# Query blocks of the causal attention from the last pair to the first, and the last product in the same order

## The chip, the cores and the metric

One core of a Trainium2 chip runs the whole program. The metric is the device time of one execution, in microseconds (us); lower is better. The engines are TensorE (PE in the profile, its weight loads PEld), VectorE (DVE), ScalarE (ACT), GpSimd (POOL) and SyncE (SP), which here only issues DMAs.

## What is computed

The program is a hybrid block for 1024 tokens of width 1024: a first block (a gated recurrence, a short convolution and a feed-forward part) and a second block with a latent attention of four heads, a pooling branch, an output product and a layer norm. The change touches only the end of the second block. Cut to that, the reference is:

```
def attend(args):                       # one block of 128 queries, all heads
    s = (einsum(qn, k_nope) + einsum(qr, k_rope)) * scale
    mask = pq[:, None, :, None] >= positions[:, None, None, :]
    p = softmax(where(mask, s, neg), axis=-1)
    return einsum(p, v)
o = lax.map(attend, (qn_b, qr_b, pos_b))
...
y_a = mla_branch(...) * silu(gate_a)
y_b = pool_branch(u_pool, pool_w, pool_scale) * silu(gate_b)
mix = concatenate([y_a, y_b], axis=-1) @ w_out
x = layer_norm(alpha * x + mix, ln_g, ln_b)
```

## The kernel before

Everything up to the attention (both input products, the recurrence, the feed-forward part, the pooling branch and its share of the output product, queries, keys and values of all heads) is left alone by the change. Products are done in three terms, with each operand split into a high and a low part.

`attention` (line 1350 and on) works for positions in order with blocks that see only what they may: query block i (128 queries) of a head sees `seen(i)` = 2 (i // 2 + 1) blocks of keys, so the eight blocks of a head are 256, 256, 512, 512, 768, 768, 1024 and 1024 keys wide. The 32 blocks of four heads are numbered n; a pair of blocks shares one tile of transposed weights. Four functions make a pipeline over n:

- `scores(n)`: five matmuls per 512 keys (three terms of the main part, two of the rotary part) into a PSUM tile; VectorE adds the mask and takes the row maximum (line 1380); ScalarE does the exponential (line 1382).
- `weights(n)`: VectorE's reciprocal of the sum (line 1387) and ScalarE's scaling (line 1388).
- `turn(n)`: one transpose per 128 keys on TensorE (line 1398), the high part by ScalarE (line 1402), the low part by VectorE (line 1403).
- `values(j)` for pair j: three matmuls of 256 columns per 128 keys, then VectorE multiplies by the gate (line 1420), ScalarE and VectorE split the result (lines 1421 and 1422).

The loop runs n from 0 to 36. At each n it issues `scores(n)`, then `values((n - 6) // 2)` at even n from 6 on, `turn(n - 3)` and `weights(n)`. At n % 8 = 1 and 5 it loads the next head's queries and keys and its gate on the SP queue, and at n % 8 = 1 and 4 of heads 1 to 3 it loads and splits rows of the output weights (lines 1446, 105 and 106; two row blocks in head 1, one in heads 2 and 3). From n = 32 on `last_product` makes the output tile of 128 tokens number t = n - 32: 24 matmuls of 512 columns over the four heads, residual and layer norm on VectorE (lines 1487 to 1494, with the small steps of lines 393 to 400), ScalarE (1495) and GpSimd (1496, 1497); the last two tiles go in halves (1500 to 1510). Residual tiles are loaded two ahead, on the SP queue.

PSUM gives four tiles of 1024 columns to all of these. The tiles of 128 x 1024 in SBUF come from a pool of 23 buffers that loads, scores and weights share. A planner orders each engine's instructions at build time from the data and buffers that it expects to be free, with the program's order as priority; the engines then run these lists in order. Masks are made for all blocks, in the order 0 to 7, before a branch on whether the positions are in order; the attention is the body of that branch.

Of the kernel before, what the change touches and what calls it, by code (L numbers as in the profile page):

```python
# [20 lines left out]
P = 128  # L21
# [34 lines left out]
def kernel(ctx: ExitStack, tc: tile.TileContext, I, out):  # L56
# [14 lines left out]
    def U(nm, dt=F32, shape=(P, 1024)):  # L71
        count[0] += 1
        return pools["u"].tile(list(shape), dt, name=f"{nm}_{count[0]}", tag="U", bufs=NU)
# [25 lines left out]
    def f(ap):  # L99
        return ap.bitcast(F32)  # L100
# [977 lines left out]
    def mm_rows(ps, y, w, t, halves=(0, 1)):  # L1078
        for n in halves:
            terms = []  # L1080
            li = (slice(None), slice(t * P, (t + 1) * P))
            ri = (slice(None), slice(n * 512, (n + 1) * 512))
            for e in range(len(y)):
                terms += three(y[e], w[e], li, ri)
            products(ps[:, n * 512:(n + 1) * 512], terms)
# [270 lines left out]
    def attention(causal):  # L1356

        N = 32
        if not causal:
            masks_all()  # L1360

        def seen(i):
            return 2 * (i // 2 + 1) if causal else NT

        sm_t, pt_t, ya, wo, Rt = {}, {}, {}, {}, {}

        def scores(n):
            h, i = divmod(n, 8)
            ps = PS("s")
            qs = (slice(None), slice(i * P, (i + 1) * P))  # L1370
            w = seen(i) * P
            for b in range((w + 511) // 512):
                ks = (slice(None), slice(b * 512, min(w, (b + 1) * 512)))
                terms = three(QN[h], KN[h], qs, ks)
                terms.append((QT[h][qs], KR["w"][0][ks]))
                terms.append((QT[h][qs], KR["w"][1][ks]))
                products(ps[ks], terms)
            s = U("sc")[:, 0:w]
            st = small("st", 4, 4)
            V.tensor_tensor_reduce(s, ps[:, 0:w], masks[causal][i][:, 0:w], 1.0, -3.0e38, ADD, MAX, st[:, 0:1])  # L1380
            V.tensor_scalar(st[:, 1:2], st[:, 0:1], -QK_SCALE, None, MUL)  # L1381
            A.activation(s, s, AF.Exp, scale=QK_SCALE, bias=st[:, 1:2], accum_out=st[:, 2:3])  # L1382
            sm_t[n] = s, st

        def weights(n):
            s, st = sm_t[n]
            V.reciprocal(st[:, 3:4], st[:, 2:3])
            A.activation(s, s, AF.Copy, scale=st[:, 3:4])  # L1388

        def turn(n):  # L1390
            s, _ = sm_t.pop(n)
            if n % 2 == 0:
                pt_t[n // 2] = HT("PT")
            pt = pt_t[n // 2]
            ps = PS("t")
            kb = seen(n % 8)
            for k in range(kb):
                PE.transpose(ps[:, k * P:(k + 1) * P], s[:, k * P:(k + 1) * P], ident)  # L1398
            v = ps.rearrange("p (k q) -> p k q", k=8)[:, 0:kb]
            hi = pt[:, 0:kb, (n % 2) * P:(n % 2 + 1) * P]  # L1400
            lo = pt[:, 0:kb, 256 + (n % 2) * P:256 + (n % 2 + 1) * P]
            A.copy(hi, v)
            V.tensor_tensor(lo, v, f(hi), SUB)  # L1403

        def values(j):
            h, q = divmod(j, 4)
            pt = pt_t.pop(j)
            ps = PS("o")
            terms = []
            for k in range(seen(2 * q)):  # L1410
                li = (slice(None), k, slice(h * P, (h + 1) * P))
                vh, vl = VV[0][li], VV[1][li]
                ph, pl = pt[:, k, 0:256], pt[:, k, 256:512]
                terms += [(vh, ph), (vh, pl), (vl, ph)]
            products(ps[:, 0:256], terms)
            qs = slice(q * 256, (q + 1) * 256)
            g = GA[h][:, qs]
            if q == 0:
                ya[h] = U("yah", F32R), U("yal", F32R)
            V.tensor_tensor(g, g, ps[:, 0:256], MUL)  # L1420
            A.copy(ya[h][0][:, qs], g)
            V.tensor_tensor(ya[h][1][:, qs], g, f(ya[h][0][:, qs]), SUB)

        def gate_load(h):
            GA[h] = U("ga")
            SY.dma_start(GA[h], GA_d[h])

        def head_load(h):
            QN[h], KN[h], QT[h] = (U("qn", F32R), U("qn", F32R)), (U("kn", F32R), U("kn", F32R)), U("qt", F32R)
            for t, src in ((KN[h][0], KN_d[h][0]), (QN[h][0], QN_d[h][0]), (KN[h][1], KN_d[h][1]),  # L1430
                           (QN[h][1], QN_d[h][1]), (QT[h], QT_d[h])):
                SY.dma_start(f(t), src)

        gate_load(0)
        for n in range(N + 5):
            if n % 8 == 1 and n // 8 < 3:
                head_load(n // 8 + 1)
            if n % 8 == 5 and n // 8 < 3:
                gate_load(n // 8 + 1)
            if n < N:  # L1440
                scores(n)
                if n % 8 == 1 and n // 8 >= 1:
                    h = n // 8
                    for e in ([0, 1] if h == 1 else [h]):
                        t = U("wo2")
                        SY.dma_start(t, w_out2[e * P:(e + 1) * P, :])
                        wo[e] = t
                if n % 8 == 4 and n // 8 >= 1:
                    h = n // 8
                    for e in ([0, 1] if h == 1 else [h]):  # L1450
                        wo[e] = split(wo[e], "wo2", of=UV if e == 0 else U)
            if n >= 6 and n % 2 == 0:
                values((n - 6) // 2)
            if 3 <= n < N + 3:
                turn(n - 3)
            if n < N:
                weights(n)
            if N - 2 <= n < N:
                t = n - (N - 2)
                Rt[t] = U("rt")  # L1460
                SY.dma_start(Rt[t], R3_d[t])
            if n == N - 2:
                gB, bB = g_bcast(I["ln_g_2"][0, :], "lng"), g_bcast(I["ln_b_2"][0, :], "lnb")
            if n >= N:
                last_product(n - N, ya, wo, Rt, gB, bB)
        for t in range(5, NT):
            last_product(t, ya, wo, Rt, gB, bB)

    def last_product(t, ya, wo, Rt, gB, bB):
        if t + 2 < NT and t + 2 not in Rt:  # L1470
            Rt[t + 2] = U("rt")
            SY.dma_start(Rt[t + 2], R3_d[t + 2])
        r = Rt[t]
        last = t >= NT - 2
        y, w = [ya[h] for h in range(4)], [wo[h] for h in range(4)]
        if t == NT - 1:
            ps = [PS("o2"), PS("o2")]
            for n in range(2):
                mm_rows(ps[n], y, w, t, (n,))
        else:  # L1480
            ps = [PS("o2")] * 2
            mm_rows(ps[0], y, w, t)
        bs = small("bs", 12, 2)
        st = small("lst", 8, 2)
        halves = [slice(0, 512), slice(512, 1024)]
        for h, hs in enumerate(halves):
            V.tensor_tensor(r[:, hs], r[:, hs], ps[h][:, hs], ADD)  # L1487
            V.bn_stats(bs[:, 6 * h:6 * h + 6], r[:, hs])
        V.bn_aggr(st[:, 0:2], bs)
        v, inv, tmp, nb = st[:, 2:3], st[:, 3:4], st[:, 4:6], st[:, 6:7]  # L1490
        V.tensor_scalar(v, st[:, 1:2], LN_EPS, None, ADD)
        if not last:
            rsqrt_col(v, inv, tmp)
            V.scalar_tensor_tensor(nb, st[:, 0:1], -1.0, inv, MUL, MUL)
            A.activation(r, r, AF.Identity, bias=nb, scale=inv)  # L1495
            G.tensor_tensor(r, r, gB, MUL)  # L1496
            G.tensor_tensor(r, r, bB, ADD)
            SY.dma_start(out[0, t * P:(t + 1) * P, :], r)
        else:
            A.activation(tmp[:, 0:1], v, AF.Sqrt)  # L1500
            V.scalar_tensor_tensor(r[:, halves[0]], r[:, halves[0]], st[:, 0:1], gB[:, halves[0]], SUB, MUL)
            newton(v, inv, tmp)
            V.scalar_tensor_tensor(r[:, halves[1]], r[:, halves[1]], st[:, 0:1], gB[:, halves[1]], SUB, MUL)  # L1503
            for hs in halves:
                if t == NT - 1:
                    V.scalar_tensor_tensor(r[:, hs], r[:, hs], inv, bB[:, hs], MUL, ADD)
                else:
                    A.activation(r[:, hs], r[:, hs], AF.Copy, scale=inv)
                    G.tensor_tensor(r[:, hs], r[:, hs], bB[:, hs], ADD)
                SY.dma_start(out[0, t * P:(t + 1) * P, hs], r[:, hs])  # L1510


    second.run(pooled_begin, lambda: kr_product(kr["w"]))
# [32 lines left out]
    with ordered.Else():  # L1546
        attention(False)
# [27 lines left out]
```

## Time and profile before

| | us |
|---|---|
| median of 3 runs | 1722.47 (1722.11 to 1723.81) |
| the profiled execution | 1726.95 |
| its span, first to last instruction | 1725.2 |
| TensorE matmul busy in it | 1627.0 (94%) |
| VectorE busy | 1195.2 (69%) |
| ScalarE busy | 777.0 (45%) |
| GpSimd busy | 359.4 (21%) |
| mean granted TensorE clock | 0.981 |

All positions in time are us from the span's start. A timeline row gives the start, the duration, the engine, the line and operation, output and input tiles with their shapes, how often, and in brackets the idle time in front with what ended it. Matmul durations overlap; how fast TensorE goes is read from the distance of their starts. The attention and the last product fill the span from about 1559 us on.

### The profile page before, as it was taken

To read this page: it belongs to the slowest core of one execution; us is meant where nothing else is said; L and a number is where in the kernel's file an instruction comes from. 1 tells how busy PE (TensorE), PEld (TensorE's weight loads), DVE (VectorE), ACT (ScalarE), POOL (GpSimd) and SP (SyncE) were. 2 spreads that over 40 slices of the span, in tenths; PEclk is the share of its full clock that TensorE was granted. 3 is DMA by queue.
4 is the path that set the end of the run, shared out by engine and by line. 5 is a ranking of instruction groups with operands and counts; after the bars stand their busy time and mean duration, and the time that the engine had idled before them with its cause. 6 is when DMAs were issued, how large, how long until landed. Compare 5 with 4: busy or idle time off the path is not lost. (4 is left out here: it accounts for less than half of the span.)

```text
span 1725.2 us, 20241 instructions
## 1 busy us (share of the span) xinstructions
PE 1627.0 (94%) x7347; PEld 1334.4 (77%) x7347; DVE 1195.2 (69%) x1765; ACT 777.0 (45%) x1147; POOL 359.4 (21%) x347
## 2 busy tenths in 40 slices
PE   5999899999999999999999999999989999988996
PEld 4777677778887787888888888888877878766885
DVE  6977676876498797767677664454877675476767
ACT  6556665762065444444444421120645344035861
POOL 1323333202032322223222000010222220030015
PEclk7999999999999999999999999999999999988998
DMA  9747566288056877877774872420387657766333
GB/s 239 136 78 140 119 122 122 46 332 205 3 149 112 191 146 153 164 148 146 142 162 93 299 269 98 104 42 2 130 159 155 140 110 269 234 195 232 110 111 112
DMA packets 272816, 255.38 MB, mean 148 GB/s; under 512 B 18398, under 2 KB 238404, under 8 KB 272708
## 3 DMA queue, kind: packets, MB, share of 16 engines
q1 hardware_dynamic: 168244, 186.80, 33.7%
q0 software_dynamic: 103744, 65.03, 26.1%
q10 hardware_dynamic: 720, 2.18, 0.3%
q8 instruction: 60, 0.98, 0.2%
q14 instruction: 48, 0.39, 0.1%
HBM read 199.56 MB, written 52.82 MB: 146 GB/s over the span
## 5 line engine op out<-in xcount | busy, mean ns | idle before, releaser
L112 PE MATMUL o<-yw 128*128 128x512 f32 x1632 | 375.9, 390 | 0.0
L112 PEld LDWEIGHTS o<-yw 128*128 128x128 f32 x1632 | 305.6, 188 | 63.7 <-DVE yw L540 0.8
L580 DVE TENSOR_TENSOR x<-x,o 128x512 f32<-128x512 f32 x160 | 108.8, 685 | 136.3 <-PE o L112 136.1
L539 ACT CAST yw<-yraw 128x1024 fp32r<-128x1024 f32 x34 | 35.7, 1051 | 194.9 <-PE o L112 176.3
L412 ACT ACTIVATE xn<-x 128x1024 f32<-128x1024 f32 x24 | 25.5, 1063 | 60.7 <-DVE x L580 54.1
L540 DVE TENSOR_TENSOR yw<-yraw,yw 128x1024 fp32r<-128x1024 f32 x34 | 41.5, 1221 | 14.9 <-ACT yw L539 14.8
L540 DVE TENSOR_TENSOR yw<-wraw,yw 128x1024 fp32r<-128x1024 f32 x34 | 41.5, 1220 | 0.8 <-ACT yw L539 0.8
L1496 POOL TENSOR_TENSOR rt<-rt,lng 128x1024 f32<-128x1024 f32 x6 | 14.4, 2403 | 122.6 <-ACT rt L1495 122.6
L775 DVE TENSOR_TENSOR ffc<-ffc,ffc 128x1024 f32<-128x1024 f32 x24 | 29.4, 1225 | 13.5 <-ACT ffc L772 13.5
L539 ACT CAST yw<-wraw 128x1024 fp32r<-128x1024 f32 x34 | 35.7, 1050 | 6.2 <-DMA wraw<-in_w_out_dram 3.2
L772 ACT ACTIVATE ffc<-ffc 128x1024 f32<-128x1024 f32 x24 | 25.5, 1062 | 25.6 <-DVE ffc L769 25.6
L441 PE MATMUL T<-cst,xn 128*128 128x128 f32 x128 | 19.6, 306 | 17.7 <-DVE ss L422 9.5
L258 POOL DMA_DIRECT2D wu3s<-in_w_in_dram x1 | 1.3, 1282 | 166.5 <-DMA wu3s<-in_w_in_dram 166.5
L1382 ACT ACTIVATE sc<-sc,st 128x256 f32<-128x256 f32 (+3 forms) x32 | 26.3, 824 | 18.9 <-DVE st L1381 18.8
L112 PE MATMUL wob<-yw 128*128 128x512 f32 x144 | 34.1, 389 | 0.0
L112 PE MATMUL o<-PT,Vh 128*128 128x256 f32 x160 | 30.0, 286 | 3.5 <-DVE PT L1403 2.9
L441 PEld LDWEIGHTS T<-cst,xn 128*128 128x128 f32 x128 | 16.5, 157 | 21.2 <-ACT hraw L456 9.9
L112 PEld LDWEIGHTS wob<-yw 128*128 128x128 f32 x144 | 27.0, 188 | 5.6
L422 POOL TENSOR_SCALAR ss<-ss 128x1 f32<-128x1 f32 x16 | 4.5, 281 | 126.0 <-ACT ss L413 125.8
L1380 DVE CUSTOM_DVE_ANT_0 sc<-s,mask 128x256 f32<-128x256 f32 (+3 forms) x32 | 25.9, 819 | 6.3 <-PE s L112 5.8
L672 POOL TENSOR_TENSOR i<-i,xc 128x1024 f32<-128x1024 f32 x8 | 21.2, 2651 | 40.7 <-ACT i L671 36.2
L1398 PE MATMUL t<-cst,sc 128*128 128x128 f32 x160 | 23.3, 277 | 6.6 <-ACT sc L1388 6.1
(1385 smaller groups left out, 4455.3 us busy)
## 6 DMA issues: line engine op xcount, KB each, us to landing
GY<-ffc SPq DMA_DIRECT2D x24, 512.0 KB
yraw<-GY SPq DMA_DIRECT2D x24, 512.0 KB
wraw<-in_w_down_dram SPq DMA_DIRECT2D x24, 512.0 KB
x<-in_x_dram SPq DMA_DIRECT2D x16, 512.0 KB
yraw<-Y SPq DMA_DIRECT2D x12, 512.0 KB
wraw<-in_w_out_dram SPq DMA_DIRECT2D x12, 512.0 KB
Y<-i SPq DMA_DIRECT2D x8, 512.0 KB
R<-x SPq DMA_DIRECT2D x8, 512.0 KB
```

The source lines that it names most:

```text
L112: PE.matmul(ps, lhsT=l, rhs=r, start=(first and j == 0), stop=(last and j == n - 1), skip_group_check=not first)
L412: A.activation(xn, X[t], AF.Square, accum_out=ss[:, 0:1])
L441: PE.transpose(ps[:, k * P:(k + 1) * P], src[:, c * P:(c + 1) * P], ident)
L539: A.copy(s[:, j], src)
L540: V.tensor_tensor(s[:, j + 1], src, f(s[:, j]), SUB)
L580: V.tensor_tensor(X[t][:, ns], X[t][:, ns], ps, ADD)
L672: G.tensor_tensor(i, i, st.pop("xc"), MUL)
L772: A.activation(st["g"], st["g"], AF.Gelu_apprx_tanh)
L775: V.tensor_tensor(st["u"], st["u"], st["g"], MUL)
L1380: V.tensor_tensor_reduce(s, ps[:, 0:w], masks[causal][i][:, 0:w], 1.0, -3.0e38, ADD, MAX, st[:, 0:1])
L1382: A.activation(s, s, AF.Exp, scale=QK_SCALE, bias=st[:, 1:2], accum_out=st[:, 2:3])
L1398: PE.transpose(ps[:, k * P:(k + 1) * P], s[:, k * P:(k + 1) * P], ident)
```

## The change

`block(n)` maps the place n % 8 in a head to the block that is done there: 6, 7, 4, 5, 2, 3, 0, 1. Scores, turns and value products take their block from it, so each head goes from its last pair of query blocks to its first. The last product takes its token tiles in the same order, and the loads of the residual and the stores of the output follow. The loop, what it issues at each n, and all shapes of a block stay as they are.

```diff
+        def block(n):
+
+            return 2 * (3 - n % 8 // 2) + n % 2
+
         def scores(n):
-            h, i = divmod(n, 8)
+            h, i = n // 8, block(n)
...
-            kb = seen(n % 8)
+            kb = seen(block(n))
...
         def values(j):
-            h, q = divmod(j, 4)
+            h, q = j // 4, 3 - j % 4
...
-            if q == 0:
+            if j % 4 == 0:
                 ya[h] = U("yah", F32R), U("yal", F32R)
...
+        def r_load(t):
+            Rt[t] = U("rt")
+            SY.dma_start(Rt[t], R3_d[block(t)])
...
             if N - 2 <= n < N:
-                t = n - (N - 2)
-                Rt[t] = U("rt")
-                SY.dma_start(Rt[t], R3_d[t])
+                r_load(n - (N - 2))
...
-                last_product(n - N, ya, wo, Rt, gB, bB)
+                last_product(n - N, block(n - N), ya, wo, Rt, r_load, gB, bB)
         for t in range(5, NT):
-            last_product(t, ya, wo, Rt, gB, bB)
+            last_product(t, block(t), ya, wo, Rt, r_load, gB, bB)

-    def last_product(t, ya, wo, Rt, gB, bB):
+    def last_product(t, i, ya, wo, Rt, r_load, gB, bB):
+
         if t + 2 < NT and t + 2 not in Rt:
-            Rt[t + 2] = U("rt")
-            SY.dma_start(Rt[t + 2], R3_d[t + 2])
+            r_load(t + 2)
...
-                mm_rows(ps[n], y, w, t, (n,))
+                mm_rows(ps[n], y, w, i, (n,))
...
-            mm_rows(ps[0], y, w, t)
+            mm_rows(ps[0], y, w, i)
...
-            SY.dma_start(out[0, t * P:(t + 1) * P, :], r)
+            SY.dma_start(out[0, i * P:(i + 1) * P, :], r)
...
-                SY.dma_start(out[0, t * P:(t + 1) * P, hs], r[:, hs])
+                SY.dma_start(out[0, i * P:(i + 1) * P, hs], r[:, hs])
```

## Rows read from the trace of the kernel before

**Rows 1.** The page, the chain that ended last, shares of the span by engine.

```profile
PE 11%; DVE 4%; ACT 1%; DMA 1%; issue 1%; POOL 0%; DVEq 0%; ACTq 0%
```

**Rows 2.** Busy time by stretch: PE, PEld, DVE, ACT, POOL, PE clock, DMA, GB/s.

```profile
1569.40:1576.00 6.60, 5.61 (x17) 4.54 (x18) 3.55 (x16) 3.15 (x10) 0.00 (x0) 0.50 1.03 416
1580.00:1660.00 80.00, 76.01 (x517) 68.57 (x516) 58.07 (x156) 65.52 (x121) 0.00 (x0) 1.00 0.20 68
1660.00:1701.00 41.00, 41.00 (x215) 35.05 (x214) 29.51 (x70) 15.08 (x22) 19.20 (x8) 1.00 0.48 167
```

**Rows 3.** Timeline of TensorE, from the last key products to the third value product.

```profile
1552.28 0.79 PE L112 MATMUL kn<-lkvh,wkvh 128*128 128x512 f32 x1 [3.19 <-DVE knl L106]
...
1555.73 0.40 PE L112 MATMUL kn<-lkvh,wkvl 128*128 128x512 f32 x1
...
1559.36 0.28 PE L112 MATMUL s<-knh,qnh 128*128 128x256 f32 x1
...
1569.47 0.69 PE L1398 MATMUL t<-cst,sc 128*128 128x128 f32 x2 [6.08 <-ACT sc L1388]
...
1579.92 0.40 PE L112 MATMUL o<-PT,Vh 128*128 128x256 f32 x2
...
1590.97 0.50 PE L112 MATMUL o<-PT,Vh 128*128 128x256 f32 x2 [1.45 <-DVE PT L1403]
```

**Rows 4.** Timeline of VectorE and ScalarE at the attention's start.

```profile
1567.42 0.42 DVE L1380 CUSTOM_DVE_ANT_0 sc<-s,mask 128x256 f32<-128x256 f32 x1 [0.56 <-DVE mask L1318]
...
1568.07 0.51 ACT L1382 ACTIVATE sc<-sc,st 128x256 f32<-128x256 f32 x1 [6.20 <-DVE st L1381]
...
1570.60 0.42 DVE L1403 TENSOR_TENSOR PT<-t,PT 128x256 fp32r<-128x256 f32 x1 [1.73 <-ACT PT L1402]
1570.94 0.41 DVE L1380 CUSTOM_DVE_ANT_0 sc<-s,mask 128x256 f32<-128x256 f32 x1
```

**Rows 5.** The chain of waits in order of time: start, us, what; whole blocks.

```profile
1577.76 2.32 PE s L112 x10
...
1593.38 0.87 PE t L1398 x8
...
1597.42 2.88 PE o L112 x24
```

**Rows 6.** Groups by line and form from 1566 us on: busy, mean ns, idle before.

```profile
L1380 DVE CUSTOM_DVE_ANT_0 sc<-s,mask 128x1024 f32<-128x1024 f32 x8 | 9.8, 1221 | 2.1 <-PE s L112 2.0
L1403 DVE TENSOR_TENSOR PT<-t,PT 128x1024 fp32r<-128x1024 f32 x8 | 9.8, 1221 | 1.9 <-ACT PT L1402 1.9
L1388 ACT ACTIVATE sc<-sc,st 128x1024 f32<-128x1024 f32 x8 | 9.2, 1146 | 0.2 <-DVE st L1387 0.2
L1382 ACT ACTIVATE sc<-sc,st 128x1024 f32<-128x1024 f32 x8 | 9.2, 1144 | 3.0 <-DVE st L1381 3.0
...
L1402 ACT CAST PT<-t 128x1024 fp32r<-128x1024 f32 x8 | 8.0, 1000 | 0.8 <-PE t L1398 0.8
...
L1403 DVE TENSOR_TENSOR PT<-t,PT 128x768 fp32r<-128x768 f32 x8 | 7.6, 952 | 0.5 <-ACT PT L1402 0.5
L1388 ACT ACTIVATE sc<-sc,st 128x768 f32<-128x768 f32 x8 | 7.5, 939 | 0.5 <-DVE st L1387 0.5
...
L1402 ACT CAST PT<-t 128x768 fp32r<-128x768 f32 x8 | 6.3, 784 | 0.0
...
L106 DVE TENSOR_TENSOR wo2l<-wo,wo2h 128x1024 fp32r<-128x1024 f32 x4 | 4.9, 1213 | 0.0
...
L105 ACT CAST wo2h<-wo 128x1024 fp32r<-128x1024 f32 x4 | 4.2, 1047 | 0.2 <-PE t L1398 0.2
```

**Rows 7.** Timeline of the tail: GpSimd and VectorE.

```profile
1703.91 2.39 POOL L1497 TENSOR_TENSOR rt<-rt,lnb 128x1024 f32<-128x1024 f32 x1
...
1704.36 1.95 DVE L398 TENSOR_TENSOR lst<-lst 128x1 f32<-128x1 f32 x1
```

**Rows 8.** The SP queue: the store of the last residual tile.

```profile
1489.65 0.34 SPq L1158 DMA_DIRECT2D RR<-rx  x1
```

## The prediction

> **What bounds the kernel now.** I read the chain of waits first: it is spread thinly, and its largest share is TensorE at 11% [rows 1], so no single place carries the kernel; only the attention and the last product are touched, so the reading goes on there alone. Next the busy time by stretch. From 1660 us to 1701 us TensorE has no idle time at all, from 1580 to 1660 it is busy 76.01 of 80 us, and from 1569.4 to 1576 its granted clock is 0.50, which is the lower of its two levels, 1.2 GHz [rows 2]. So this stage is bound by TensorE with two leaks: a start that costs much, and 4.0 us of gaps later. The timeline of TensorE shows both. It begins the scores at 1559.36 and waits 6.08 us at 1569.47 for the first softmax; and the third value product of the next head waits 1.45 us at 1590.97 for the split weights [rows 3]. The timeline of VectorE says why the start is late: the first score block is read at 1567.42, behind the masks and the branch, and nothing that this change moves lies ahead of that [rows 4].
>
> **What the change does to the work.** Each head has eight score blocks, of widths 256, 256, 512, 512, 768, 768, 1024, 1024. After the change the widest come first. Nothing is added or removed: the instructions of a head are the same ones in another order, on every engine. I take four places.
>
> **A, the start.** The milestone is the first value product, 1579.92 in the trace [rows 3]. In program order seven score blocks and three turns (the transposes) stand ahead of it in both kernels. A widest score block is ten matmuls in 2.32 us, eight transposes take 0.87, a value product of 24 takes 2.88 [rows 5]; the other sizes go in proportion, so scores cost 0.58, 1.16, 1.74, 2.32 and turns 0.22, 0.44, 0.66, 0.87. Before: 2 x 0.58 + 2 x 1.16 + 2 x 1.74 + 2.32 + 2 x 0.22 + 0.44 = 10.2 us of work, so 1579.92 - 1559.36 - 10.2 = 10.4 us are lost. After: 2 x 2.32 + 2 x 1.74 + 2 x 1.16 + 0.58 + 2 x 0.87 + 0.66 = 13.4 us of work ahead of the same milestone. When does that come? VectorE reads block 0 from 1567.42 as before. There, from that start of 0.42 us to the exponential is 0.65 us [rows 4]; with 1.22 for the wide block [rows 6] it is 1.45, so ScalarE begins at 1568.87. Ahead of the value product it does two wide exponentials (1.14), two wide scalings (1.15), two exponentials and a scaling of width 768 (0.94 each, by the scaling's row) and two splits (1.00) [rows 6]: 2.28 + 2.30 + 2.82 + 2.00 = 9.4 us, to 1578.3; VectorE's low part of the second block, 1.22, ends at 1579.5. Lost: 1579.5 - 1559.36 - 13.4 = 6.7 us. Gain 10.4 - 6.7 = 3.7 us. TensorE fills its early wait with scores that run on to about 1559.36 + 8.1 = 1567.5, and then idles some 4 us instead of 6.08; an idle time of 3.19 us was already enough for the lower clock at 1552.28 [rows 3], so I count on slow matmuls here too, and they fit: from 1571.5 to 1579.5 stand 5.3 us of work. The upper end of the gain is 4.6: the exponential of the fourth block gives way, 0.94 us. The lower end is 0.5, and it hangs on the order in which VectorE was given its work. In the trace it sat idle 1.73 us and did the low part of block 0 at 1570.60, and only then block 1, at 1570.94 [rows 4], though that block's scores had long been made. If this order is kept, block 0 is through only at about 1575.6 (1571.5, transposes at the lower clock 1.75, split 1.00, low part 1.22, issue), block 1 needs 1.45 + 1.14 + 0.3 + 1.15 + 0.87 + 1.00 + 1.22 = 7.1 more, the milestone is 1582.7 and the gain 10.4 - 9.9 = 0.5. I take 3.7, because that idle time holds a place for block 1 once block 0 takes twice as long.
>
> **B, the later heads.** The 4.0 us of gaps between 1580 and 1660 [rows 2] come where a value product finds its weights unsplit. Before, the tightest is the third pair (width 768): between its turn and its product TensorE has 0.58 + 0.87 + 1.16 = 2.6 us of other work, against a split of 0.78 and a low part of 0.95 [rows 6]; it waited 1.45, so 2.6 + 1.45 - 1.73 = 2.3 us of queue lay in front. After, the tightest is the widest pair, four steps into its head: 1.16 + 0.66 + 0.58 = 2.4 us of cover against 1.00 + 1.22 = 2.2. With the same queue it would wait 2.1, with none 0. The queue is shorter (a 512-wide exponential and a gate copy, where a 1024-wide scaling stood), so I take 1.5 us of it: a wait of 1.3, three times (heads 1 to 3; head 0 is in A): 3.9 - 4.0 = -0.1 us. Ends: -4.0 (no waits) and 3 x 2.1 - 4.0 = +2.3. The splitting of the output weights stands in the same step of a head, now a thin one, and is counted in a rival.
>
> **C, the end of the attention.** At step 32 the value product of the third-to-last pair (768 wide) follows its turn by one narrow score block and one turn only, 0.58 + 0.44 = 1.0 us, as no scores are left; it needs 0.78 + 0.95 = 1.7 and some handing over. I take +1.0, between 0 (other products fill it) and 2.0. Before, this place held a narrow pair and 2.32 us of scores, and no gap [rows 2].
>
> **D, the tail.** The last product takes the tiles in the new order with the same shapes, so its cost is unchanged: TensorE has no gap there [rows 2]. Behind it VectorE's small multiply (line 398) waits on a running GpSimd instruction, 1.95 us at 1704.36 while one of 2.39 us ran from 1703.91 [rows 7]; the pace of the tiles ahead of that shifts, so this can be 1.9 us less or 2.4 more, and I take 0. The loads of the residual tiles on the SP queue are the same eight in the same places; the last of those tiles was stored at 1489.65 [rows 8], so which one comes first costs nothing.
>
> Sum: -3.7 - 0.1 + 1.0 + 0 = -2.8 us. Against the profiled execution's own 1726.95 that is 1724.15; on the median, 1722.47 - 2.8 = 1719.7 us. The two differ by 4.5 us before, so I carry the difference, not the level.
>
> **The rivals.** *Gaps gone* (faster): the widest pair comes while two wide score blocks of its own head still cover it, and C is filled by the last product: A and B at -3.7 and -4.0, C at 0, -7.7 us, 1714.8. For it: ScalarE is busy 65.5 of 80 us [rows 2], so it has room when the load is level. Against: its load is not level, the 2.4 us of cover is the thinnest of either order. *Start unchanged*: VectorE keeps block 1 behind block 0's low part, as in the trace [rows 4]; A is -0.5 and the sum +0.4, 1722.9: the change then does not do what it could. *Thin step* (slower): the splitting of the output weights, 1.05 on ScalarE and 1.21 on VectorE [rows 6], falls in front of the widest pair's split in each of heads 1 to 3. A wait is then 1.3 + 1.05 + 1.21 = 3.6 us, B is 3 x 3.6 - 4.0 = +6.7, the sum +4.0, 1726.5. It decides from 2.2 us a head, where 3 waits eat 4.0 + 3.7 - 1.0. *Thin step and a slow clock*: if these waits reach the 3.19 us behind which the trace shows the lower clock, each is followed by what 1552.28 to 1555.73 shows, eight matmuls in 3.45 us where they take 1.86 at full clock, 1.6 us more [rows 3, 5]. B is 3 x (3.2 + 1.6) - 4.0 = +10.4, the sum +7.7, 1730.2. Against it: after the wait of 1.45 us the clock stayed at 1.00 [rows 2, 3].
>
> On that last one the Trainium skill, page "TensorE: Matmul & The Clock Gate", section "HAM oscillation — how this bites in real kernels", speaks against the change: idle stretches that return between bursts of matmuls let the clock be throttled each time, and every burst pays the slow beginning again. By that rule the time would be the 1730.2 of this rival if the waits are long enough; by the row of 1.45 us they cost only themselves.
>
> **How the numbers follow.** Forecast 0.38, gaps gone 0.26, start unchanged 0.16, thin step 0.14, thin step with slow clock 0.06. A measurement of this kernel can tell about 0.2%, 3.4 us, from no change, so the bounds are 1719.0 and 1725.9. The forecast's own spread (1.5 us, mostly A's and D's) puts a third of it under 1719.0: faster 0.26 + 0.12 = 0.38, slower 0.20, same 0.42. The range runs from 1714.0 to 1727.0, over all but the slow clock and the edges of the others; the forecast's own is 1717.5 to 1722.
>
> **What would show it.** A: the first value product near 1579.5 with 13.4 us of work ahead of it, and VectorE reading block 1 before block 0's low part. B: one wait of about 1.3 us in each later head, on the low part of the widest pair. C: about 1 us between the last turns. D: VectorE's tail behind the last matmul as long as now, some 13 us. The prediction is wrong if the weight splits queue ahead of the widest pair, if the waits reach 2.2 us a head, or if TensorE's clock falls after the start.

## The result, and the profile after

The changed kernel took 1738.76 us (median of 4 runs, 1733.71 to 1739.61) beside 1722.29 us (median of 4, 1721.38 to 1723.81) for the kernel before. The measured ratio is 1.0080, with a 95% interval of 1.0064 to 1.0096; the quotient of the two medians, 1.0096, lies at the upper end of it. The change is slower by 0.8%, where 1719.7 us and a range up to 1727.0 were forecast.

The profiled execution of after took 1733.71 us (span 1731.9, mean granted clock 0.976), 6.8 us more than the one of before. That difference is not the cost of the change. After began its first score at 1553.62, before at 1559.36 [rows 3], and no part of the change lies ahead of that point. In the runs of the experiments, the kernel before itself ranged from 1720.6 to 1735.4 us (two executions of it, at mean granted clocks of 0.745 and 0.839, took 2055.4 and 1845.2 us and are left out). So from here on I compare *stages*: from the first score matmul to the end of the span, in each profile. In that measure the same waits come back with the same length, to a tenth or two of a us, in every kernel that leaves the place alone. What does not come back alike is how long the granted clock stays low at the start. In the old order it is back at 1.00 between 14.7 us (e4, below) and 17.9 us (e6) after the first score, 16.7 in before; in the new one between 20.3 us (e5) and 23.7 us (e9), 21.7 in after. Where two kernels differ only in steps behind the matmuls, the part up to the last matmul still differs by 0.5 to 0.8 us (after and e5, e1 and e9, e4 and e10, before and e8, in the table of experiments). So differences of stages under about 1 us are not read as effects.

| us | before | after |
|---|---|---|
| first score matmul to last matmul's start | 152.01 | 162.09 |
| last matmul's start to the end (tail) | 13.83 | 16.19 |
| stage | 165.84 | 178.28 |

The stage grew by 12.4 us: 10.1 on TensorE's side and 2.4 in the tail. That lies inside the measured interval of the whole time (+11.0 to +16.5 us). What the medians differ by beyond it, some 4 us, the profiles do not place.

The page's chain of waits, shares of the span by engine, still names no single place; TensorE's share went from 11% [rows 1] to 12%:

```profile
PE 12%; DVE 4%; ACT 2%; issue 1%; DMA 0%; POOL 0%; DVEq 0%; ACTq 0%
```

Busy time by stretch of after (us, then PE, PEld, DVE, ACT, POOL with their counts, granted clock, DMA share, GB/s), to be laid beside [rows 2]:

```profile
1569.40:1576.00 6.60, 4.54 (x19) 3.58 (x18) 2.15 (x9) 6.60 (x12) 0.00 (x0) 0.55 0.52 197
1600.00:1610.00 10.00, 5.14 (x31) 4.76 (x30) 6.35 (x14) 8.03 (x16) 0.00 (x0) 0.83 0.00 0
1610.00:1620.00 10.00, 10.00 (x68) 9.12 (x67) 5.90 (x15) 6.23 (x12) 0.00 (x0) 1.00 0.68 254
1630.00:1640.00 10.00, 6.88 (x37) 6.55 (x36) 4.97 (x11) 5.64 (x10) 0.00 (x0) 0.67 0.16 52
1640.00:1650.00 10.00, 10.00 (x64) 8.93 (x63) 7.43 (x20) 7.04 (x15) 0.00 (x0) 0.99 0.19 55
1650.00:1660.00 10.00, 9.78 (x69) 8.80 (x67) 7.61 (x23) 9.09 (x14) 0.00 (x0) 1.00 0.00 1
1670.00:1700.00 30.00, 30.00 (x144) 25.17 (x143) 21.89 (x49) 8.54 (x15) 14.24 (x6) 1.00 0.49 177
```

Two of these stretches carry the loss. From 1600 to 1610 TensorE is busy 5.14 us and from 1630 to 1640 6.88 us, and in both the granted clock is below 1.00. Before had 1.00 from 1580 to 1660 [rows 2]. The stretches between and behind them are full or nearly so.

The timeline of all engines in these two places (start, duration, engine, line and operation, tiles and shapes, count; in brackets the idle time in front and what ended it). The lines of weights and turns have moved by four against the kernel before: 1402 is the turn, 1406 and 1407 its high and low part:

```profile
1601.56 1.98 ACT L105 CAST wo2h<-wo 128x1024 fp32r<-128x1024 f32 x2
1602.62 2.36 DVE L106 TENSOR_TENSOR wo2l<-wo,wo2h 128x1024 fp32r<-128x1024 f32 x2 [0.77 <-ACT wo2h L105]
1603.74 1.00 ACT L1406 CAST PT<-t 128x1024 fp32r<-128x1024 f32 x1
1605.23 1.22 DVE L1407 TENSOR_TENSOR PT<-t,PT 128x1024 fp32r<-128x1024 f32 x1
1606.51 0.79 PE L112 MATMUL o<-PT,Vh 128*128 128x256 f32 x2 [4.86 <-DVE PT L1407]
...
1610.74 0.49 PE L1402 MATMUL t<-cst,sc 128*128 128x128 f32 x3
...
1630.55 1.03 ACT L105 CAST wo2h<-wo 128x1024 fp32r<-128x1024 f32 x1
1631.62 1.23 DVE L106 TENSOR_TENSOR wo2l<-wo,wo2h 128x1024 fp32r<-128x1024 f32 x1 [0.77 <-ACT wo2h L105]
1631.80 1.00 ACT L1406 CAST PT<-t 128x1024 fp32r<-128x1024 f32 x1
1633.10 1.22 DVE L1407 TENSOR_TENSOR PT<-t,PT 128x1024 fp32r<-128x1024 f32 x1
1634.46 0.77 PE L112 MATMUL o<-PT,Vh 128*128 128x256 f32 x2 [3.12 <-DVE PT L1407]
...
1639.72 0.58 PE L1402 MATMUL t<-cst,sc 128*128 128x128 f32 x2
```

Read the two groups from top to bottom. On ScalarE, and then on VectorE, the splitting of the output weights (wo2h, wo2l) is done ahead of the split of the widest pair's second block (PT), which TensorE is waiting for. Each of the two engines works its list in order, and VectorE even idles 0.77 us for wo2h with the PT step standing behind it. TensorE's value product of 24 matmuls then waits 4.86 us in head 1, where two row blocks are split, and 3.12 us in head 2, where there is one. And the product itself is slow: 1606.51 to 1610.74 is 4.23 us and 1634.46 to 1639.72 is 5.26 us, where it takes 2.88 at full clock [rows 5].

### The profile page after: what moved, and what is told of

Same layout as the page of the kernel before. It is cut to its first block, busy times and chain, and to the rows that moved or that the text cites. A ratio compares the mean times of both kernels' runs of the same rounds, so it can differ in the third digit from the quotient of the medians.

```text
span 1731.9 us, 20245 instructions
## 1 busy us (share of the span) xinstructions
PE 1632.6 (94%) x7347; PEld 1339.6 (77%) x7347; DVE 1202.8 (69%) x1765; ACT 777.4 (45%) x1147; POOL 359.0 (21%) x347
## 5 line engine op out<-in xcount | busy, mean ns | idle before, releaser
L112 PE MATMUL o<-PT,Vh 128*128 128x256 f32 x160 | 33.7, 307 | 9.5 <-DVE PT L1407 9.3
L112 PEld LDWEIGHTS o<-PT,Vh 128*128 128x128 f32 x160 | 28.4, 212 | 11.4 <-DVE PT L1407 7.0
L441 PE MATMUL T<-cst,xn 128*128 128x128 f32 x128 | 20.1, 310 | 16.9 <-ACT ws0op L267 9.4
L1386 ACT ACTIVATE sc<-sc,st 128x1024 f32<-128x1024 f32 (+3 forms) x32 | 26.3, 824 | 21.0 <-DVE st L1385 19.2
L1407 DVE TENSOR_TENSOR PT<-t,PT 128x1024 fp32r<-128x1024 f32 (+3 forms) x32 | 26.1, 820 | 8.0 <-ACT PT L1406 7.8
L1384 DVE CUSTOM_DVE_ANT_0 sc<-s,mask 128x1024 f32<-128x1024 f32 (+3 forms) x32 | 26.1, 820 | 6.6 <-PE s L112 6.0
```

The source lines that it names most:

```text
L112: PE.matmul(ps, lhsT=l, rhs=r, start=(first and j == 0), stop=(last and j == n - 1), skip_group_check=not first)
L441: PE.transpose(ps[:, k * P:(k + 1) * P], src[:, c * P:(c + 1) * P], ident)
```

## The experiments

All times are stages as above, each from one profile, unless a ratio is given; a ratio is to the kernel before on the same chip, with its 95% interval. Kernels with "one run" have no ratio.

| kernel | first score to last matmul | tail | stage | ratio |
|---|---|---|---|---|
| before | 152.01 | 13.83 | 165.84 | 1 |
| after | 162.09 | 16.19 | 178.28 | 1.0080 |
| e1, weight splits moved | 153.31 | 15.80 | 169.11 | 1.0018 [0.9999, 1.0037] |
| e2, only heads 1 and 2 reversed | 156.31 | 13.81 | 170.12 | 1.0029 [1.0006, 1.0052] |
| e3, only head 0 reversed | 156.26 | 14.08 | 170.34 | 1.0042 [1.0021, 1.0062] |
| e4, only head 3 and the tiles reversed | 151.49 | 16.17 | 167.66 | 1.0033 [1.0009, 1.0057] |
| e5, after with small steps rewritten | 161.39 | 13.13 | 174.52 | one run |
| e6, before with splits moved | 151.76 | 13.82 | 165.58 | one run |
| e7, e1 with a later first split | 154.91 | 15.91 | 170.82 | one run |
| e8, before with small steps rewritten | 152.46 | 13.24 | 165.70 | 1.0006 [0.9992, 1.0019] |
| e9, e1 and e5 together | 154.04 | 12.81 | 166.85 | 0.9998 [0.9982, 1.0014] |
| e10, e4 and e5 together | 152.26 | 13.13 | 165.39 | 0.9988 [0.9972, 1.0003] |

**e1: the weight splits away from the thin step.** In the changed kernel, one line:

```diff
-                if n % 8 == 4 and n // 8 >= 1:
+                if n % 8 == 7 and n // 8 >= 1:
```

> The changed kernel, with the splitting of the output weights moved three steps on, from n % 8 = 4 to n % 8 = 7, behind the widest pair's value product. Theory 1 (the splits stand in front of the widest pair's own split): the waits of 4.9 and 3.1 us at the third head's turn fall under 1.5 us, the granted clock stays at 1.00 from 1590 us on, and 8 to 11 us come back: about 1725 to 1730 us. Rival (the cover of 2.4 us is too thin by itself, splits or not): the waits stay above 3 us and the time within 3 us of the changed kernel's 1738.8.

The stage fell by 9.2 us, from 178.28 to 169.11. The widest pair of head 1, in the timeline of e1:

```profile
1603.26 1.00 ACT L1406 CAST PT<-t 128x1024 fp32r<-128x1024 f32 x1
1604.29 1.22 DVE L1407 TENSOR_TENSOR PT<-t,PT 128x1024 fp32r<-128x1024 f32 x1 [0.30 <-ACT PT L1406]
1604.32 0.39 PE L112 MATMUL o<-PT,Vh 128*128 128x256 f32 x1 [1.26 <-ACT PT L1406]
```

and its busy time by stretch there:

```profile
1604.00:1610.00 6.00, 5.47 (x42) 5.14 (x43) 4.34 (x7) 5.76 (x12) 0.00 (x0) 1.00 0.03 3
```

With no weight split in front, the wait is 1.26 us (and 0.22 more behind it) instead of 4.86, head 2's is 0.67 and 0.57 instead of 3.12, and the granted clock stays 1.00. What the theory expected (waits under 1.5 us, the clock at 1.00, 8 to 11 us back) came, and the rival, that the cover is too thin with or without the splits, fell. The place of the splits is the cause of most of the loss, shown by moving them alone.

**e2, e3, e4: one place of the change at a time.** The order is reversed only for the heads in a list:

```diff
-            return 2 * (3 - n % 8 // 2) + n % 2
+            return 2 * (3 - n % 8 // 2) + n % 2 if n // 8 in (1, 2) else n % 8
...
-            h, q = j // 4, 3 - j % 4
+            h, q = j // 4, block(2 * j) // 2
```

with (0,) in e3 and (3,) in e4; the last product's tiles follow head 3.

> The kernel before, with heads 1 and 2 alone from the last pair to the first; heads 0 and 3 and the last product as before. Theory 1 puts most of the loss here: 6 to 12 us slower than before, 1728 to 1734. Rival (the loss is spread over the start, the heads and the tail alike): 2 to 5 us slower.

> The kernel before, with head 0 alone from the last pair to the first. By the trace of the changed kernel the start lost 11.6 us against 10.4 before: 0 to 2 us slower than before. By the prediction's term A it would be 3.7 us faster.

> The kernel before, with head 3 alone from the last pair to the first, and the last product in that order. Theory: the value products leave the stretch of the last product, its tiles come every 5.4 to 6 us, and VectorE with its waits on GpSimd falls behind: 13.6 us between the last matmul and the end become 15.5 to 16.5, and with some 1 us of waits in head 3 it is 2 to 4 us slower than before. Rival (the tail is the same, the loss lies in the heads alone): at most 1 us slower, and 13.6 us stay 13.6.

The stages grew by 4.3, 4.5 and 1.8 us: 10.6 together, where the whole change costs 12.4. Three expectations on the sizes missed. Theory 1 put 6 to 12 us on heads 1 and 2, and the 4.3 of e2 lies in its rival's 2 to 5. Head 0 was to cost 0 to 2 us and cost 4.5, and e4's 1.8 is under its 2 to 4. So the sum comes near, but not place by place. Head 1 waits only 2.31 us in e2, with the same two row blocks split ahead of it. The difference that e2 keeps is head 0 in the old order, whose last value product, just ahead of this place, has 24 matmuls (2.88 us) instead of 6 (0.72); that these 2.2 us make most of the 2.55 us of difference is argued, not shown. The timeline of e2, and under it its busy time by stretch (the granted clock is the third number from the end):

```profile
1610.97 0.50 PE L112 MATMUL o<-PT,Vh 128*128 128x256 f32 x2 [2.31 <-DVE PT L1407]
```

```profile
1611.00:1612.10 1.10, 1.10 (x9) 1.10 (x10) 1.10 (x3) 0.00 (x0) 0.00 (x0) 1.00 0.00 0
1612.10:1615.30 3.20, 3.20 (x18) 3.20 (x18) 1.17 (x7) 2.32 (x6) 0.00 (x0) 0.52 0.00 0
```

Even a wait of 2.31 us was followed by the lower of the two clock levels, 1.1 us after the matmuls had begun again. In e3 the shape of the loss is another. The reversed head 0 is followed by a head 1 in the old order, and that head waits 0.98, 2.07 and 1.85 us (timeline, and busy time by stretch under it):

```profile
1609.95 0.63 PE L1402 MATMUL t<-cst,sc 128*128 128x128 f32 x4 [2.07 <-DVE st L1384]
...
1620.86 0.50 PE L112 MATMUL o<-PT,Vh 128*128 128x256 f32 x2 [1.85 <-DVE PT L1407]
```

```profile
1609.90:1613.00 3.10, 3.05 (x16) 2.49 (x17) 2.88 (x9) 2.39 (x5) 0.00 (x0) 1.00 0.00 0
1620.80:1624.00 3.20, 3.14 (x27) 3.14 (x28) 2.87 (x10) 1.62 (x5) 0.00 (x0) 1.00 0.26 101
```

The clock stayed at 1.00 there. This change from the new order to the old does not occur in after, where head 1 is reversed too, so e3 does not price the start alone, and that the three sum to near 12.4 is partly chance. In e4, TensorE's part is 0.5 us shorter than before, which the start explains: its clock was back 2.0 us earlier, and its first value product came 19.77 us after the first score instead of 20.56. The waits add up to 10.9 us in e4 and 11.0 in before. The tail of e4 is that of after, 16.17 us, as its theory expected. So the longer tail belongs to the order of head 3 and the tiles, and to nothing ahead of it.

**e6: the same place in the old order.** The kernel before with the splits issued at n = 16 (two row blocks), 24 and 28:

```diff
-                if n % 8 == 4 and n // 8 >= 1:
-                    h = n // 8
-                    for e in ([0, 1] if h == 1 else [h]):
+                if n in (16, 24, 28):
+                    for e in {16: [0, 1], 24: [2], 28: [3]}[n]:
```

> The kernel before, in its own order, with the splitting of the output weights moved from the fifth block of a head to the first block of the next (n = 16, 24; the last at 28), which is the thin step of that order. Theory 1 (the place of the splits in front of a tight pair's own split does the damage, not the order of the blocks): TensorE's waits of 1.45 us at the second and 0.6 us at the third change of heads grow to 2.5 to 4 us each, 3 to 6 us from the first score to the end, more if the clock falls. Rival (only the widest pair suffers): less than 1 us.

No wait of before grew by more than 0.02 us, and the 1.45 us of head 1's third pair are gone. The tightest place of head 0 is as in [rows 3]:

```profile
1591.05 0.50 PE L112 MATMUL o<-PT,Vh 128*128 128x256 f32 x2 [1.44 <-DVE PT L1403]
```

The waits behind it are 0.26, 0.50 and 0.51 us, and the stage is 165.58. But the edit moved only two of the four splits in time. ScalarE began them at 1596.03, 1610.80, 1636.38 and 1645.22; in before at 1595.94, 1598.67, 1625.45 and 1645.89, so the planner left the first and the last where they were. The two that moved (1610.80 and 1636.38) stand near the third pairs of heads 1 and 2, each with one row block, and those pairs did not wait longer. So that a split stands in a step with little cover was not enough by itself in these two places. The general form of the theory fell there, on one profile; two row blocks in one such step of the old order were not tried. What e1 shows holds for the reversed order.

**e7: the first split behind the second exponential.** e1, and in head 0 only:

```diff
+            if n == 0:
+                with tc.issue_after(exps[1]):
+                    A.copy(hi, v)
+            else:
+                A.copy(hi, v)
```

> The changed kernel with the weight splits at n % 8 = 7, and ScalarE's high part of block 0 queued behind the exponential of block 1 instead of ahead of it. Theory for the start (in the changed kernel ScalarE sat 2.06 us in front of that high part while block 1 waited): the first value product comes 1 to 2.5 us earlier after the first score than the 25.0 us of the run with the splits moved. Rival (the start is set by the slow clock and by the amount of work on ScalarE): within 0.5 us of 25.0.

The second matmul of the first value product came 26.58 us after the first score, 1.6 later than in e1 (25.01), so theory and rival both missed. The two profiles also differ in the clock, as the busy time by stretch shows from 21.2 to 24.3 us after the first score (e1, then e7):

```profile
1576.49:1579.59 3.10, 2.69 (x21) 2.32 (x20) 1.96 (x8) 2.85 (x6) 0.00 (x0) 1.00 0.69 190
1583.88:1586.98 3.10, 3.10 (x13) 2.70 (x12) 1.66 (x3) 2.33 (x4) 0.00 (x0) 0.50 0.49 172
```

The clock was low until 24.4 us in e7 and until 21.1 in e1. Between after and e5, whose starts are the same program, a low clock until 21.7 instead of 20.3 us goes with a first value product at 25.26 instead of 24.14 us. So the 1.6 us are no measure of the edit. The gain of 1 to 2.5 us did not show; that ScalarE's order plays no part at all is not shown.

**e5 and e8: the small steps at the end.** The Newton steps of the layer norm (one number for each of 128 tokens) take two operands from SBUF. Written with one, and the other as a column of scalars, in after (e5) and in before (e8):

```diff
-        V.tensor_tensor(tmp[:, 1:2], out, v, MUL)
-        V.scalar_tensor_tensor(tmp[:, 1:2], tmp[:, 1:2], -0.5, out, MUL, MUL)
-        V.scalar_tensor_tensor(out, tmp[:, 1:2], 1.5, out, ADD, MUL)
+        V.tensor_scalar(tmp[:, 1:2], out, v, None, MUL)
+        V.tensor_scalar(tmp[:, 1:2], tmp[:, 1:2], -0.5, out, MUL, MUL)
+        V.tensor_scalar(out, tmp[:, 1:2], 1.5, out, ADD, MUL)
...
-            V.scalar_tensor_tensor(nb, st[:, 0:1], -1.0, inv, MUL, MUL)
+            V.tensor_scalar(nb, st[:, 0:1], -1.0, inv, MUL, MUL)
```

> The changed kernel, with the four small steps of the layer norm (lines 398 to 400 and the bias) written with one operand from SBUF and the other as a column of scalars, in place of two operands from SBUF. Theory for the tail (VectorE's two-operand steps wait out GpSimd instructions, up to 2.2 us a tile, so its tiles come every 6.4 us where TensorE's come every 5.4): those steps take 0.15 to 0.2 us each, the tiles follow TensorE's pace, and the time from the last matmul to the end falls from 16.2 us to 13.8 or less. Rival (the tail is long because the value products left it and VectorE has simply too much to do): it stays above 15.5 us.

> The kernel before with the same small steps as in e5_after_ts. By the theory for the tail the waits of 1.95 us and the like leave its chain too: 1.5 to 3 us from the last matmul to the end are saved, 13.8 to 11 or 12, and the time falls by as much. Rival (the tail's end is set by the large two-operand steps of the last two tiles): less than 1 us.

First the tail of after. Rows 1493 are VectorE's first step on a tile, two halves; rows 398 and 400 are small steps:

```profile
1691.64 1.69 DVE L398 TENSOR_TENSOR lst<-lst 128x1 f32<-128x1 f32 x1
1693.83 1.28 DVE L1493 TENSOR_TENSOR rt<-rt,o 128x512 f32<-128x512 f32 x2
1698.06 2.16 DVE L398 TENSOR_TENSOR lst<-lst 128x1 f32<-128x1 f32 x1
1700.72 1.28 DVE L1493 TENSOR_TENSOR rt<-rt,o 128x512 f32<-128x512 f32 x2
1704.63 2.39 POOL L1503 TENSOR_TENSOR rt<-rt,lnb 128x1024 f32<-128x1024 f32 x1
1704.79 2.24 DVE L400 SCALAR_TENSOR_TENSOR lst<-lst 128x1 f32<-128x1 f32 x1
1707.15 1.29 DVE L1493 TENSOR_TENSOR rt<-rt,o 128x512 f32<-128x512 f32 x2
1711.23 2.24 DVE L400 SCALAR_TENSOR_TENSOR lst<-lst 128x1 f32<-128x1 f32 x1
1713.68 1.28 DVE L1493 TENSOR_TENSOR rt<-rt,o 128x512 f32<-128x512 f32 x2
```

In each of these tiles one small step is held until a GpSimd instruction that began ahead of it ends (1704.63 and 1704.79, both to about 1707.03). VectorE's tiles come every 6.43 to 6.89 us with no idle time in front, where the 24 matmuls of a tile take TensorE 5.4. VectorE is the slower one here, and falls behind. In e5, the same steps beside the same GpSimd work:

```profile
1707.51 0.21 DVE L398 TENSOR_SCALAR lst<-lst 128x1 f32<-128x1 f32 x1
1707.98 2.41 POOL L1503 TENSOR_TENSOR rt<-rt,lnb 128x1024 f32<-128x1024 f32 x1
1708.01 0.22 DVE L400 TENSOR_SCALAR lst<-lst 128x1 f32<-128x1 f32 x1
1709.22 1.29 DVE L1493 TENSOR_TENSOR rt<-rt,o 128x512 f32<-128x512 f32 x2 [0.75 <-PE o L112]
```

They take 0.21 us, VectorE waits for TensorE again, and the tail is 13.13 us instead of 16.19; the rival, over 15.5 us, fell. The Trainium skill, page "SBUF — State Buffer", section "Who interferes with whom", says that VectorE and GpSimd share one pair of ports to SBUF, which one of them locks while the other waits; the rows agree (2.24 us beside GpSimd with two operands from SBUF, 0.22 with one). In the kernel before, the same edit moved the tail only from 13.83 to 13.24 us, and the time not measurably: the theory's 1.5 to 3 us missed, and the rival's "less than 1 us" came. There the last two value products, of 18 and 24 matmuls (from 1672.98 and 1686.94), stand among the tiles, and VectorE catches up beside them: in before it idles 2.24 us at a tile's first step, while the four tiles of after shown above have no idle time in front. The timeline of VectorE in before:

```profile
1695.47 1.28 DVE L1487 TENSOR_TENSOR rt<-rt,o 128x512 f32<-128x512 f32 x2 [2.24 <-PE o L112]
```

In the new order these two products have 12 and 6 matmuls (from 1680.89 and 1693.43), 24 fewer; at 0.12 us each (24 in 2.88 [rows 5]) that is 2.9 us. The two turns among the tiles have also shrunk, from eight transposes each to two. From the first matmul of the last product to the last, TensorE took 50.3 us in before (1661.04 to 1711.37) and 46.1 in after (1669.62 to 1715.71), so VectorE had 4.2 us less for the same eight tiles. The tail grew by 2.4. e4 and e5 show where the longer tail comes from and that the held steps carry it; that the lost cover sets its size is argued from these rows.

**e9 and e10: the parts put together.** e9 is after with the edits of e1 and e5, e10 is e4 with that of e5.

> The changed order with two edits together: the splits of the output weights moved to the last pair of each head (as in e1_split7), and the Newton steps of the last LayerNorm written with one operand in SBUF and a scalar column (as in e5_after_ts). Theory: the loss of the change is made of three parts that don't touch each other, the start, the thin step of heads 1 and 2, and the steps that wait for GpSimd at the end. Then the two edits add: the part from the first score to the last matmul stays that of e1 (153.3 us), the tail is that of e5 (13.1 us), the stage 166.4 us, level with the kernel before (165.8), ratio within 0.3% of 1. Rival: with the weights' splits late in each head VectorE reaches the last stage later and the tail stays at 15 us or more: stage 168 to 169 us, as e1 alone.

> Only head 3's blocks and the last product's token tiles in the reversed order, with the Newton steps written with one operand in SBUF. Theory: head 3's order takes away the waits of 1.4, 0.5 and 0.6 us late in the attention (e4: 151.5 us from the first score to the last matmul against 152.0 before), and its tail of 16.2 us falls to some 13.2 us once the steps no longer wait for GpSimd: stage 164.7 us, 1.1 us (0.07%) below the kernel before, which a comparison can hardly tell from 1. Rival: e4's tail grew because the value products that stood between the token tiles are gone, whatever the steps cost: tail 15 to 16 us, stage 167 us.

The edits add: e9's stage is 166.85 us, against 166.4 expected, and its time can't be told from that of the kernel before. Two small edits take back 11.4 of the 12.4 us. e10 came to 165.39 (164.7 expected; its waits of 1.45, 1.45, 0.37 and 0.61 us are those of e4, and its part up to the last matmul is 0.8 us longer than e4's, as its clock at the start was back at 16.7 us, not 14.7). The interval of its ratio, 0.9988, includes 1: a gain over the kernel before is not shown for any order.

## Why the prediction was wrong

**What held.** The reading of what bounds the stage held: TensorE, with the start and the tight pairs as leaks. So did the list of what would make the forecast wrong, and all three points on it came: the weight splits queued ahead of the widest pair, waits over 2.2 us in two heads, and a clock that fell after the start. The rival *thin step and a slow clock* named the mechanism with its place, and gave it 0.06.

**B, the step that failed.** The forecast put 1.5 us of queue in front of the widest pair's split, worked out from what stood in front of a *different* pair in the old order (the 1.45 us at 1590.97 are the third value product of head 0, not "of the next head"), and set the weight splits apart as a rival. But where they stand could be read. At n % 8 = 4 the loop issues the weight splits, then a value product, then `turn(n - 3)`, and in the new order that turn is the widest pair's second block. The splits are the next wide work ahead of it on ScalarE and on VectorE. They belonged in the sum. The rest of B was well sized: with the splits moved away, e1's waits in heads 1 to 3 are 3.5 us, where three times 1.3 were forecast. Measured, heads 1 to 3 waited 4.86, 3.12 and 0.25 + 0.28 = 8.5 us, against 4.0 us of gaps before [rows 2]; the slow products add (4.23 - 2.88) + (5.26 - 2.88) = 3.7. B is +8.2, where -0.1 was forecast and the rival had +10.4. The rival's even three times 3.2 us was wrong: two row blocks cost more than one, and head 3 hardly paid. There ScalarE began the weight split at 1657.35, 1.62 us ahead of TensorE's next turn (1658.97); in head 2 it began 0.80 us behind the same turn (1630.55 and 1629.75). So the split was out of the way in time, and TensorE lost 0.53 us in two waits. ScalarE's list was another there: in head 2 a scaling of width 768 and an exponential of 512 stand ahead of the weight split (1629.01 and 1629.85), in head 3 they come behind the widest pair's split (1659.20 and 1660.03). Why the planner ordered head 3 so is not settled by a run.

The argument against the slow clock was one row: after 1.45 us the clock had stayed at 1.00 [rows 2, 3]. That bounds the danger from one side only. The next row above was 3.19 us, with the slow clock behind it, and all between was unknown. The rival's waits of 3.6 us lay above both, so once the splits are in front of the widest pair the slow clock follows, and most of the chance of the thin step belonged to it. It did fall, behind 3.12 and 4.86 us.

**A, mis-sized: +0.7 instead of -3.7.** The rows of after at the start, on all engines:

```profile
1553.62 0.39 PE L112 MATMUL s<-knh,qnh 128*128 128x512 f32 x1
...
1561.71 1.22 DVE L1384 CUSTOM_DVE_ANT_0 sc<-s,mask 128x1024 f32<-128x1024 f32 x1 [0.59 <-PE s L112]
1564.52 1.21 DVE L1384 CUSTOM_DVE_ANT_0 sc<-s,mask 128x1024 f32<-128x1024 f32 x1
1565.84 1.97 PE L1402 MATMUL t<-cst,sc 128*128 128x128 f32 x8 [4.05 <-ACT sc L1392]
1567.85 1.01 ACT L1406 CAST PT<-t 128x1024 fp32r<-128x1024 f32 x1 [2.06 <-PE t L1402]
1568.75 1.15 ACT L1386 ACTIVATE sc<-sc,st 128x1024 f32<-128x1024 f32 x1
1568.89 1.23 DVE L1407 TENSOR_TENSOR PT<-t,PT 128x1024 fp32r<-128x1024 f32 x1 [1.27 <-ACT PT L1406]
1572.00 1.97 PE L1402 MATMUL t<-cst,sc 128*128 128x128 f32 x8 [2.06 <-ACT sc L1392]
1576.88 0.28 PE L112 MATMUL o<-PT,Vh 128*128 128x256 f32 x1
1577.56 0.87 PE L1402 MATMUL t<-cst,sc 128*128 128x128 f32 x6 [0.41 <-DVE st L1384]
1578.88 0.39 PE L112 MATMUL o<-PT,Vh 128*128 128x256 f32 x1 [0.44 <-DVE PT L1407]
```

What was forecast here came in three of its steps. VectorE read the first block 8.09 us after the first score (8.06 in before [rows 3, 4]). It read the second block ahead of the first one's low part, at 1564.52, long before 1568.89. TensorE's first wait was 4.05 us ("some 4 us instead of 6.08"). The step that failed is the sum of ScalarE's work, 9.4 us back to back. ScalarE waited 2.06 us at 1567.85 for the transposes, eight in 2.0 us at the lower clock, and did the second block's exponential only behind the first one's split; TensorE waited 2.06 us again. The first value product began at 23.26 us after the first score, not 20.1; the lower bound of A had 1582.7 - 1559.36 = 23.3. A single matmul of it was done, and the rest waited until 25.26 us. With the one more turn of 0.66 us and the matmul that had been done by then, 14.2 us of work lie ahead of that point, so 11.1 us are lost against 10.4. In waits the two starts are equal: 6.08 + 0.92 = 7.0 us in before, 4.05 + 2.06 + 0.41 + 0.44 = 7.0 in after; the rest is matmuls at the lower clock. So the forecast's gain in waits did not come: the second wait of 2.06 us took back what the first one had lost. The runs also gave each start other clocks. With the reversed head 0, the point of 25.26 us lies at 24.14 (e5) to 25.71 (e9); in the old order, the first value product's 20.56 us lies at 19.77 (e4) to 21.09 (e6). The means of the five and of the six profiles put A at +0.5, and where the clock was back early in both (e5 and e4) it is +0.3. So +0.7 is no exact size, but even the lowest pairing (e5 and e6) is -1.0, far from -3.7. As e7 showed no gain, what is left is the chain exponential, scaling, transposes, split, low part of a wide block in series. That is argued from the rows.

**C, right in kind:** a wait of 0.61 us at the end of the attention, +1.0 forecast.

**D, mis-sized: +2.4 instead of 0.** The mechanism had been seen: a small step of VectorE held by GpSimd for 1.95 us [rows 7]. The step that failed is "its cost is unchanged". It counted the matmuls of the tiles, which are the same, and not the value products between them, beside which VectorE had caught up; +2.4 was the upper end given.

Sum of what was measured: 0.7 + 8.2 + 0.6 + 2.4 = 11.9 of the stage's 12.4 us. Half a microsecond is not placed; two profiles of kernels that are alike up to the last matmul differ by as much.

## What to carry to other kernels

When blocks of different width change places, go through everything that the loop hangs on a step number (weight splits, loads, gate copies) and ask which block it now stands in front of; in-order queues make that the first term of the sum, not a rival. Give filler work a step where nothing urgent stands behind it, as e1 did with one line for 9.2 us. And count cover at both ends: the wide work that moves to the front is also gone from the end, where a slower engine was using it to catch up. And when a planner orders the work, look in the trace where an edit has put it: in e6 two of four splits did not move.

## What the runs showed of the hardware

- TensorE's granted clock stayed at 1.00 behind waits of 1.45 (before), 1.85 and 2.07 us (e3), and fell to its lower level behind waits of 2.31 (e2), 3.12 and 4.86 us (after). The Trainium skill, page "TensorE: Matmul & The Clock Gate", section "HAM oscillation — how this bites in real kernels", describes such loss behind returning waits; here a wait of 2.31 us, well short of the 3.19 us of [rows 3], was already followed by it: 24 matmuls in 4.29 us (1610.97 to 1615.26) instead of 2.88.
- At the start of the attention the granted clock came back to 1.00 at different times in executions of the same order: 20.3 us after the first score in e5, 21.7 in after, 23.7 in e9, with the first value product (its second matmul) at 24.14, 25.26 and 25.71 us.
- A step of 128 x 1 elements on VectorE, 0.16 us alone, lasted up to 2.24 us beside GpSimd when it had two operands in SBUF, and 0.21 to 0.22 with one of them as a scalar column.
